# A hybrid decoder layer on one core: tables earlier, squares on one engine, factors spread by matmul

## The chip, the cores and the metric

The kernel runs on one core of a Trainium2 chip. What is compared is the device time of one launch in microseconds (us). The core has TensorE (PE in the profile; its weight loads are PEld), VectorE (DVE), ScalarE (ACT), GpSimd (POOL) and SyncE (SP), each with its own queue of instructions that run in the order in which they stand. SP and ScalarE also issue the DMAs.

## The reference

One layer over x (2048 rows of 1024 fp32 numbers): RMS norm, one input projection, three kinds of heads, a gate, an output projection, a second RMS norm and the residual. Cut to what matters here:

```python
def rmsnorm(x, g):
    xf = x.astype(jnp.float32)
    xf = xf * lax.rsqrt(jnp.mean(xf * xf, axis=-1, keepdims=True) + EPS)
    return (xf * g.astype(jnp.float32)).astype(x.dtype)
...
    h = rmsnorm(x, g_pre[i])
    proj = h @ w_in[i]
    val, gate = proj[..., :MIX_W], proj[..., MIX_W:]
    y_pool = pool_mixer(u_pool, w_pool[i], pool_scale[i])
    y_ssm = s5_mixer(u_ssm, a_re[i], a_im[i], log_dt[i], b_re[i], b_im[i],
                     c_re[i], c_im[i], d_skip[i], w_glu[i])
    y_att = memory_attention(q, mem, g_mem[i], w_kv[i])
    y = jnp.concatenate([y_pool, y_ssm, y_att], axis=-1) * jax.nn.silu(gate)
    x = x + rmsnorm(y @ w_out[i], g_post[i])
```

The pool heads take running means over 2, 4, 8 or 16 rows. The scan heads (`s5_mixer`) run a linear recurrence with 64 complex states for each of 24 groups; its powers and angles are tables made from a_re, a_im and log_dt. The attention heads read 256 memory rows, which are normed, too.

## The kernel before, in words

Every product is made from split operands: a number is the sum of a rounded high part (ScalarE, line 159) and the rest (VectorE or GpSimd, line 160), and `mm3` (lines 162 to 165) makes three multiplications of them. x is not divided by its root mean square ahead of the products. The row factors are made apart, and each product is multiplied by them when it leaves PSUM (`qf` of line 904, `gp` of 999, `up` of 1031), so that products can run before the factors are known.

The rows come in four chunks of 512. The first stage (to about 107 us) makes, for each chunk, the scan heads' part of the projection (`u_mm`, product `pu`), empties it (`us`) and stores it to DRAM (`ud`). Between these stand the keys and values of the memory (`kv_mm`, products `pkv`), the parameter tables (`param_tables`), the pool heads' weights folded into the projection's (`pool_fold`: a product `pf` in one of the two banks tagged mm, the copy `wpo` of line 358, a store to `wpd`), and the squares of all rows of x. `row_squares` (line 187) loads x again in 32 pieces of 128x512 and squares them with a sum along each row, the first half of each row tile on ScalarE and the second on VectorE.

`rstd_out` (line 223) makes the factors of all 2048 rows on VectorE (`row_rstd`, thirteen small steps, lines 170 to 203), turns them with one TensorE transposition (`rs_t`, line 227), and stores them to DRAM twice, in row order (`rsd`) and in the scan's order (`rsp`). `rs_load` then loads 512 of them into all 128 partitions (`rs_b`), and `rs_ct_load` loads the scan's copy (`rs_ct`). For the memory's rows another way is in use: `rstd_spread` (line 207) multiplies a column of factors, repeated 128 times, with the identity matrix, which leaves the factors along the free axis on all partitions, and ScalarE copies them out of PSUM.

`param_tables` works on all three elementwise engines: VectorE makes exponentials, GpSimd two halves of a table of angles in turns (`ph`, lines 472 to 479, in buffers that both halves share), VectorE its absolute value (`rd`, line 480), ScalarE sines and cosines (lines 484 and 485), VectorE from these `XT_` and `YT_` (lines 490 and 491).

The second stage (from about 107 to 515 us) runs through the queries (`pjq`), pool heads (`pjp`) and gates (`pjg`) of each half of the rows, in the two banks tagged mm. The steps of attention and of twelve scan blocks are put between them; a scan block's first product is `pa`, its inputs `uh` and `ul` come from `ur`, which GpSimd multiplies by `rs_ct`, and its last product `py` needs `hh` and `hl`. The third stage is the output projection.

The order is not that of the program. A scheduler with a timing model of its own places each engine's instructions, taking those that stand earlier in the program first where several could go. A line moved in the program so changes priorities, and with them the order of everything behind it.

The lines of the main sequence that the change touches, each on a line of its own in the listing:

```python
    kv_mm(1, wkv[1])
    wkv.append(kv_weight(3))
...
    row_squares(ssq_m, mem, range(NMEM // P), "rsm")
    kv_mm(2, wkv[2])
...
    vfs = kv_values(pkv[1], rm)
    param_tables()
...
    rstd_out()
    rs_load(0)
    rs_load(1)
    rs_ct_load()
```

Of the kernel before, what the change touches and what calls it, by code (L numbers as in the profile page):

```python
# [10 lines left out]
F32 = mybir.dt.float32  # L11
F32R = mybir.dt.float32r
I32 = mybir.dt.int32
AF = mybir.ActivationFunctionType
# [4 lines left out]
P = 128  # L19
# [63 lines left out]
def hybrid_layer_kernel(  # L83
# [53 lines left out]
    def aux_bank(name, shape=(P, CH)):  # L137
        return psum.tile(list(shape), F32, tag="aux", name=name, bufs=6)
# [49 lines left out]
    def row_squares(ss, rows, tiles, name):  # L188

        for i in tiles:  # L190
            for h in range(2):
                xr = t2k(f"{name}_x{i}_{h}")
                dma(xr, rows[i * P:(i + 1) * P, h * CH:(h + 1) * CH])
                if h:
                    dve.scalar_tensor_tensor(
                        xr, xr, 1.0, xr, op0=ALU.mult, op1=ALU.mult, accum_out=ss[:, h, i:i + 1]
                    )
                else:
                    act.activation(xr, xr, AF.Square, accum_out=ss[:, h, i:i + 1])

    def row_rstd(ss, nt, name):
        sm = small.tile([P, nt], F32, tag=f"rsu{nt}", name=f"{name}_sum", bufs=1)
        dve.tensor_tensor(sm, ss[:, 0, :], ss[:, 1, :], op=ALU.add)
        return rstd_from(sm, nt, name)

    def rstd_spread(r, n, dst, name):

        bc = aux_bank(f"{name}_bc", (P, n))
        for i in range(n // P):
            pe.matmul(  # L210
                bc[:, i * P:(i + 1) * P], r[:, i:i + 1].broadcast_to([P, P]), ident, start=True, stop=True
            )
        act.activation(dst, bc, AF.Copy)
# [9 lines left out]
    def rstd_out():  # L223

        r = row_rstd(ssq_x, NTT, "rs")
        rt_ = aux_bank("rs_t", (NTT, P))
        pe.transpose(rt_, r, ident)
        ro = small.tile([NTT, 2, P], F32, tag="rs_o", name="rs_o", bufs=1)
        act.activation(ro[:, 0, :], rt_, AF.Copy)
        act.activation(  # L230
            ro[:, 1, :].rearrange("i (s j) -> i s j", s=T),
            rt_.rearrange("i (j s) -> i s j", s=T)[:, ::-1, :],
            AF.Copy,
        )
        store(rsd, ro[:, 0, :])
        store(rsp.rearrange("s i j -> i s j"), ro[:, 1, :].rearrange("i (s j) -> i s j", s=T))

    def rs_load(c):
        rs_b[c] = const.tile([P, CH], F32, tag="rs_b", name=f"rs_b{c}", bufs=2)
        dma(rs_b[c], rsd[c * CH // P:(c + 1) * CH // P, :].rearrange("i p -> (i p)").partition_broadcast(P))  # L240
# [305 lines left out]
    def kv_weight(m, raw=None):  # L546
        return w_tile(w_kv[:, m * P:(m + 1) * P], f"wkv{m}", raw)

    def kv_mm(m, w):
        if m % 2 == 0:  # L550
            pkv[m // 2] = mm_bank(f"pkv{m // 2}", (P, 2, NMEM))
        o = pkv[m // 2][:, m % 2, :]
        for k in range(KT):
            mm3(o, w[0][:, k, :], w[1][:, k, :], mems[k][:, 0, :], mems[k][:, 1, :], k == 0, k == KT - 1)
# [55 lines left out]
    u_evac(2)  # L610
    kv_mm(0, wkv[0])
    wkv.append(kv_weight(2, ph1a))
    kv_mm(1, wkv[1])
    wkv.append(kv_weight(3))
    u_store(2)
    u_mm(3, [0])
    load_chunk(0, False)
    row_squares(ssq_m, mem, range(NMEM // P), "rsm")
    kv_mm(2, wkv[2])
    u_evac(3, [0])  # L620
    u_mm(3, [1])
    param_loads()
    rm_ = row_rstd(ssq_m, NMEM // P, "rsm")
    kv_mm(3, wkv[3])
    u_evac(3, [1])
# [10 lines left out]
    rstd_spread(rm_, NMEM, rm, "rsm")  # L636
    kv_keys(pkv[0], rm)
    vfs = kv_values(pkv[1], rm)
    param_tables()
    u_mm(0, [2])  # L640
    u_evac(0, [2])
    u_mm(1, [0])
# [5 lines left out]
    u_evac(1, [1])  # L648
    u_mm(1, [2], between=folds)
    rstd_out()  # L650
    rs_load(0)
    rs_load(1)
    rs_ct_load()
    u_evac(1, [2])
    u_store(1)
# [751 lines left out]
```

## Time and profile before

| | |
|---|---|
| median of 3 runs | 755.06 us (754.26 to 757.27) |
| the profiled execution's own time | 754.54 us |
| its span | 752.8 us |
| mean granted clock of TensorE | 0.98 |
| busy: TensorE, its weight loads | 708.1 us (94%), 575.9 us (77%) |
| busy: VectorE, ScalarE, GpSimd | 525.7 (70%), 337.4 (45%), 364.1 us (48%) |

The profiled execution is one run of the program; it lies 0.52 us below the median. Busy time is an average over stages with different limits. Where a row of the trace ends with square brackets, they hold the time for which the engine did nothing before this instruction, and what ended that.

### The profile page before, as it was taken

What the parts mean: (1) busy time and instruction counts of PE and PEld (TensorE: products, weight loads), DVE (VectorE), ACT (ScalarE), POOL (GpSimd) and SP (SyncE); (2) the same over time, 40 slices, a digit from 0 to 9 for tenths busy, and PEclk for the clock granted to TensorE, in tenths of its full rate; (3) what the DMA queues carried; (4) which work ended last, traced back from release to release, by engine and by line L of the source; (5) the groups of instructions that cost most, each with busy time, mean ns of one, the idle gap of its engine ahead of it and who ended that gap; (6) DMA issues with size and microseconds to landing.
All of it is one profiled execution on the core that took longest, in us unless ns stands there. A gap on an engine that the chain in (4) does not pass through costs nothing.

```text
span 752.8 us, 10077 instructions
## 1 busy us (share of the span) xinstructions
PE 708.1 (94%) x3449; PEld 575.9 (77%) x3449; DVE 525.7 (70%) x901; ACT 337.4 (45%) x731; POOL 364.1 (48%) x311
## 2 busy tenths in 40 slices
PE   6999787999979799888999999999999999999996
PEld 5788676887858588666888888888887888888885
DVE  4699594689889887978788978657606964343224
ACT  5675432557455453445555565447632524221111
POOL 0049852678758566846858488103042621421121
PEclk9999998999999899999999999999999999999999
DMA  7998985233333347482332324377725464330331
GB/s 252 309 328 270 336 288 156 98 108 126 121 114 119 112 150 247 161 280 83 122 107 71 121 81 154 134 224 275 226 80 192 130 199 123 113 126 14 112 113 56
DMA packets 95268, 121.03 MB, mean 161 GB/s; under 512 B 31585, under 2 KB 63025, under 8 KB 95217
## 3 DMA queue, kind: packets, MB, share of 16 engines
q1 hardware_dynamic: 82320, 90.08, 38.1%
q10 hardware_dynamic: 12896, 30.30, 10.6%
q8 instruction: 27, 0.44, 0.2%
q14 instruction: 25, 0.20, 0.1%
HBM read 81.68 MB, written 38.68 MB: 160 GB/s over the span
## 4 chain that ended last, share of the span: by engine, by line
PE 59%; DVE 13%; ACT 3%; issue 2%; DMA 1%; ACTq 0%; POOL 0%; DVEq 0%; POOLq 0%
PE pout L165 8%; PE pout L164 8%; PE pout L163 8%; PE pjg L163 5%; PE pjg L164 5%; PE pjg L165 5%; PE pz L163 2%; PE pz L165 2%; PE pz L164 2%; PE pjp L163 2%; PE pjp L164 2%; PE pjp L165 2%; DVE gg L847 2%; DMA ysd<-ys 1%; DVE yt L1007 1%
## 5 line engine op out<-in xcount | busy, mean ns | idle before, releaser
L163 PE MATMUL pjg<-xh,wg_h 128*128 128x512 f32 x256 | 103.6, 405 | 0.0
L164 PE MATMUL pout<-wol,yh 128*128 128x512 f32 (+1 forms) x264 | 102.0, 386 | 0.0
L164 PE MATMUL pjg<-xl,wg_h 128*128 128x512 f32 x256 | 101.9, 398 | 0.0
L165 PE MATMUL pjg<-xh,wg_l 128*128 128x512 f32 x256 | 101.7, 397 | 0.0
L163 PE MATMUL pout<-woh,yh 128*128 128x512 f32 (+1 forms) x264 | 101.6, 386 | 0.0
L165 PE MATMUL pout<-woh,yl 128*128 128x512 f32 (+1 forms) x264 | 101.2, 387 | 0.0
L1217 POOL TENSOR_TENSOR ov<-ov,xres 128x1024 f32<-128x1024 f32 x15 | 36.7, 2444 | 126.8 <-DVE ov L1216 105.0
L1213 ACT ACTIVATE ov<-pout 128x512 f32<-128x512 f32 x30 | 17.9, 596 | 105.3 <-PE pout L165 82.0
L163 PEld LDWEIGHTS pjg<-xh,wg_h 128*128 128x128 f32 x256 | 48.5, 189 | 12.8 <-issue 1.6
L164 PEld LDWEIGHTS pout<-wol,yh 128*128 128x128 f32 x264 | 49.5, 188 | 11.0
L163 PEld LDWEIGHTS pout<-woh,yh 128*128 128x128 f32 x264 | 49.5, 188 | 10.9
L165 PEld LDWEIGHTS pout<-woh,yl 128*128 128x128 f32 x264 | 49.5, 188 | 10.9
L165 PEld LDWEIGHTS pjg<-xh,wg_l 128*128 128x128 f32 x256 | 48.4, 189 | 11.3
L164 PEld LDWEIGHTS pjg<-xl,wg_h 128*128 128x128 f32 x256 | 48.7, 190 | 10.1
L160 POOL TENSOR_TENSOR yl<-yb,yh 128x512 fp32r<-128x512 f32 x20 | 26.9, 1375 | 60.6 <-ACT yh L159 39.7
L254 DVE SCALAR_TENSOR_TENSOR xl<-xr,gpre,xh 128x512 fp32r<-128x512 f32 x48 | 43.0, 908 | 18.7 <-ACT xh L253 18.6
L844 POOL TENSOR_TENSOR v<-v,ax 128x512 f32<-128x512 f32 x12 | 16.8, 1403 | 68.0 <-DVE ax L843 50.8
L253 ACT ACTIVATE xh<-xr,gpre 128x512 fp32r<-128x512 f32 x48 | 33.2, 715 | 32.4 <-DMA xr<-in_xT_dram 10.3
L163 PE MATMUL pu<-xh,wsh 128*128 128x512 f32 x96 | 39.0, 421 | 8.2 <-ACT wsh L159 6.8
L1185 DVE SCALAR_TENSOR_TENSOR ow<-ssq,ov 128x1 f32<-128x1 f32 x16 | 2.7, 168 | 54.7 <-ACT ov L1213 54.6
L163 PE MATMUL pjp<-xh,wp_h 128*128 128x512 f32 x96 | 39.0, 407 | 0.7 <-DVE gp L999 0.7
L164 PE MATMUL pu<-xl,wsh 128*128 128x512 f32 x96 | 38.7, 416 | 0.3 <-DVE xl L254 0.3
(300 smaller groups left out, 1929.3 us busy)
## 6 DMA issues: line engine op xcount, KB each, us to landing
xr<-in_xT_dram SPq DMA_DIRECT2D x32, 256.0 KB
rs_x<-in_x_dram SPq DMA_DIRECT2D x32, 256.0 KB
yd<-yt ACTq DMA_DIRECT2D x16, 512.0 KB
xres<-in_x_dram SPq DMA_DIRECT2D x16, 512.0 KB
out_dram<-ov SPq DMA_DIRECT2D x15, 512.0 KB
yb<-yd SPq DMA_DIRECT2D x20, 256.0 KB
wg_r<-in_w_in_dram SPq DMA_DIRECT2D x8, 512.0 KB
wsh<-wg_h ACTq DMA_DIRECT2D x8, 512.0 KB
```

Source lines behind the costliest of these rows:

```text
L160: sub.tensor_tensor(lo, src, hi.bitcast(F32), op=ALU.subtract)
L163: pe.matmul(ps, ahi, bhi, start=first, stop=False)
L164: pe.matmul(ps, ahi, blo, start=False, stop=False)
L165: pe.matmul(ps, alo, bhi, start=False, stop=last)
L253: act.activation(h, xr, AF.Copy, scale=gpre[:, k:k + 1])
L254: dve.scalar_tensor_tensor(l, xr, gpre[:, k:k + 1], h.bitcast(F32), op0=ALU.mult, op1=ALU.subtract)
L844: pool.tensor_tensor(v, v, ax, op=ALU.add)
L847: dve.tensor_tensor_scan(gg[:, i, :], r8[:, g0 + i:g0 + i + 1].broadcast_to([P, NJ]), v[:, i, :], 0.0, op0=ALU.mult, op1=ALU.add,)
L1007: dve.scalar_tensor_tensor(o, branch()[:, cc * CH:(cc + 1) * CH], 0.5, th, op0=ALU.mult, op1=ALU.mult)
L1185: dve.scalar_tensor_tensor(w, ssq[:, i:i + 1], 1.0 / D, v, op0=ALU.mult, op1=ALU.add)
L1213: act.activation(ov[:, HALVES[n]], ps[n], AF.Square, accum_out=ssq[:, n:n + 1])
L1217: pool.tensor_tensor(ov, ov, xr, op=ALU.add)
```

## The change

It does three things. `param_loads` and `param_tables` stand earlier in the program: the loads between the two products of the keys, the tables ahead of the values' first product. All squares are made by ScalarE, those of the memory's rows too. And the factors of chunks 0 and 1 are no longer loaded from DRAM but spread by `rstd_spread`, with four multiplications each, into the same tiles `rs_b`. The stores to DRAM stay, as the scan's copy and chunks 2 and 3 are still loaded from there.

```diff
@@ row_squares
                 dma(xr, rows[i * P:(i + 1) * P, h * CH:(h + 1) * CH])
-                if h:
-                    dve.scalar_tensor_tensor(
-                        xr, xr, 1.0, xr, op0=ALU.mult, op1=ALU.mult, accum_out=ss[:, h, i:i + 1]
-                    )
-                else:
-                    act.activation(xr, xr, AF.Square, accum_out=ss[:, h, i:i + 1])
+                act.activation(xr, xr, AF.Square, accum_out=ss[:, h, i:i + 1])
@@ rstd_out
         r = row_rstd(ssq_x, NTT, "rs")
+        for c in range(2):
+            rs_b[c] = const.tile([P, CH], F32, tag="rs_b", name=f"rs_b{c}", bufs=2)
+            rstd_spread(r[:, c * CH // P:(c + 1) * CH // P], CH, rs_b[c], f"rs{c}")
         rt_ = aux_bank("rs_t", (NTT, P))
@@ main sequence
     wkv.append(kv_weight(2, ph1a))
+    param_loads()
     kv_mm(1, wkv[1])
...
     row_squares(ssq_m, mem, range(NMEM // P), "rsm")
+    param_tables()
     kv_mm(2, wkv[2])
     u_evac(3, [0])
     u_mm(3, [1])
-    param_loads()
...
     vfs = kv_values(pkv[1], rm)
-    param_tables()
     u_mm(0, [2])
...
     rstd_out()
-    rs_load(0)
-    rs_load(1)
     rs_ct_load()
```

On TensorE 8 multiplications are new; ScalarE has 20 instructions more, VectorE 18 squares fewer, SP two loads fewer. What the scheduler makes of it shows at three places. The names with the last number taken as a buffer's are those of the program: `rd`, `ph`, `sin`, `cos` here belong to the second half of the tables.

VectorE around the second half of the tables, where the first folded weights (`wpo`) leave PSUM; before:

```order
L195 SCALAR_TENSOR_TENSOR rs_x_1_791,ssq_x<-rs_x_1_791 128x512
L195 SCALAR_TENSOR_TENSOR rs_x_1_797,ssq_x<-rs_x_1_797 128x512
L583 TENSOR_TENSOR vhl<-vt_1130,vhl 128x2x64
L583 TENSOR_TENSOR vhl<-vt_1137,vhl 128x2x64
L480 SCALAR_TENSOR_TENSOR rd_994<-ph_993 128x492
L583 TENSOR_TENSOR vhl<-vt_1130,vhl 128x2x64
L491 SCALAR_TENSOR_TENSOR YT__114<-sin_975,yk 128x216
L583 TENSOR_TENSOR vhl<-vt_1137,vhl 128x2x64
L358 COPY wpo_1156<-pf_1151 128x384
L490 TENSOR_TENSOR XT__113<-cos_976,yk 128x216
```

and with the change:

```order
L565 TENSOR_TENSOR vf_1050<-pkv_703,rm 128x256
L160 TENSOR_TENSOR kl<-kf_1044,kh 128x256
L478 SCALAR_TENSOR_TENSOR rd_645<-ph_644 128x492
L489 SCALAR_TENSOR_TENSOR YT__114<-sin_626,yk 128x216
L581 TENSOR_TENSOR vhl<-vt_1130,vhl 128x2x64
L581 TENSOR_TENSOR vhl<-vt_1137,vhl 128x2x64
L488 TENSOR_TENSOR XT__113<-cos_627,yk 128x216
L356 COPY wpo_1156<-pf_1151 128x384
```

The squares ahead of `rd` are gone, and the first `wpo` has moved behind `XT_`, which needs the cosines.

ScalarE at the same place, with the change (`rs_x` are the squares; before, six stood ahead of the sines, and they were every other one):

```order
L194 ACTIVATE rs_x_0_931,ssq_x<-rs_x_0_931 128x512
L194 ACTIVATE rs_x_1_934,ssq_x<-rs_x_1_934 128x512
L482 ACTIVATE sin_626<-ph_644 128x108
L482 ACTIVATE SIN<-ph_644,cs 128x384
L194 ACTIVATE rs_x_0_937,ssq_x<-rs_x_0_937 128x512
L580 ACTIVATE vhl<-vt_1130 128x2x64
L580 ACTIVATE vhl<-vt_1137 128x2x64
L483 ACTIVATE cos_627<-rd_645,cs 128x108
L483 ACTIVATE COS<-rd_645,cs 128x384
```

Eight squares stand ahead of the sines now, and 24 behind them.

TensorE at the end of the first query weight's products (`pjq`), where the factors come in; before:

```order
L164 MATMUL pjq_0_1_1412<-xl_5_724,wq_0_h 128x512
L227 MATMUL rs_t<-ident,rs_y_1284 16x128
L165 MATMUL pjq_0_1_1412<-xh_5_723,wq_0_l 128x512
...
L165 MATMUL pjq_0_1_1412<-xh_7_735,wq_0_l 128x512
L745 MATMUL pr_1338<-ident,rt_1331 128x128 x2
L754 MATMUL pk_1345<-ox_1326,rt_1331 16x128 x2
L163 MATMUL pjq_0_0_1495<-xh_0_488,wq_0_h 128x512
```

and with the change:

```order
L165 MATMUL pjq_0_1_1422<-xh_6_872,wq_0_l 128x512
L205 MATMUL rs_bc<-ident,rs_y_1284 128x128 x8
L225 MATMUL rs_t<-ident,rs_y_1284 16x128
L163 MATMUL pjq_0_1_1422<-xh_7_878,wq_0_h 128x512
L164 MATMUL pjq_0_1_1422<-xl_7_879,wq_0_h 128x512
L165 MATMUL pjq_0_1_1422<-xh_7_878,wq_0_l 128x512
L741 MATMUL pr_1348<-ident,rt_1341 128x128 x2
L750 MATMUL pk_1355<-ox_1336,rt_1341 16x128 x2
L163 MATMUL pjq_0_0_1505<-xh_0_502,wq_0_h 128x512
```

The eight new multiplications and the transposition stand four multiplications later, after 21 of the 24 of this product; the second query weight's first product still follows the first scan block's kernel (`pr`, `pk`).

## Rows read from the trace of the kernel before

**Rows 1.** Stretches: length, busy us of PE, PEld, DVE, ACT, POOL; clock, DMA share, GB/s
```profile
84.00:109.00 25.00, 19.13 (x103) 16.12 (x102) 19.94 (x45) 9.37 (x28) 13.88 (x14) 0.93 0.99 342
60.00:160.00 100.00, 90.21 (x445) 73.61 (x444) 74.24 (x127) 44.38 (x107) 65.80 (x62) 0.95 0.65 214
160.00:260.00 100.00, 89.26 (x480) 72.00 (x479) 90.64 (x119) 52.00 (x129) 72.21 (x59) 0.95 0.38 129
```

**Rows 2.** Whom TensorE waited for, 60 to 160 us (total, times, longest)
```profile
PE pf L356 <- DVE wpo L358: 4.3, 2, 3.9
PE pjq L163 <- DVE qf L904: 3.9, 1, 3.9
PE pjq L163 <- DVE wpo L358: 1.6, 1, 1.6
```

**Rows 3.** The stretches after the two long waits (columns as in rows 1)
```profile
91.30:95.20 3.90, 3.90 (x14) 3.33 (x15) 3.90 (x9) 2.40 (x7) 3.60 (x4) 0.57 1.06 377
123.40:129.30 5.90, 5.90 (x14) 4.66 (x15) 3.63 (x4) 1.86 (x3) 1.27 (x1) 0.50 0.80 268
```

**Rows 4.** VectorE in order of time (start, us, instruction; idle before it)
```profile
67.84 2.17 DVE L160 TENSOR_TENSOR wq_l<-wq_r,wq_h 128x1024 fp32r<-128x1024 f32 x1
69.93 1.08 DVE L304 COPY us<-pu 128x512 f32<-128x512 f32 x1
...
89.40 0.67 DVE L480 SCALAR_TENSOR_TENSOR rd<-ph 128x492 f32<-128x492 f32 x1 [4.94 <-POOL ph L479]
```

**Rows 5.** GpSimd in order of time, the second half of the tables
```profile
71.66 1.41 POOL L472 TENSOR_TENSOR ph<-fa,cs 128x492 f32<-128x492 f32 x1 [1.35 <-DVE rd L480]
...
76.16 1.41 POOL L522 TENSOR_TENSOR Bre<-br,cr 128x384 f32<-128x384 f32 x1
77.53 0.84 POOL L526 TENSOR_TENSOR Bim<-bi,cr 128x384 f32<-128x384 f32 x1
...
88.15 1.22 POOL L479 TENSOR_TENSOR ph<-ph,rd 128x492 f32<-128x492 f32 x1
```

**Rows 6.** The squares of x rows (ns min/median/max, first and last start)
```profile
L199 ACT ACTIVATE rs_x<-rs_x x16: 614/630/634, 75.3 to 107.5; 128x512 f32<-128x512 f32 x16
L195 DVE SCALAR_TENSOR_TENSOR rs_x<-rs_x x16: 668/758/1531, 76.2 to 107.0; 128x512 f32<-128x512 f32 x16
```

**Rows 7.** TensorE in order of time, the waits and the transposition
```profile
91.28 1.51 PE L356 MATMUL pf<-wp,wpt 96*128 96x96 f32 x8 [3.95 <-DVE wpo L358]
...
116.80 0.27 PE L227 MATMUL rs_t<-ident,rs_y 128*16 128x128 f32 x1
...
123.39 0.80 PE L163 MATMUL pjq<-xh,wq_h 128*128 128x512 f32 x1 [3.92 <-DVE qf L904]
```

**Rows 8.** VectorE in order of time, the factor chain's first and last
```profile
108.70 0.68 DVE L203 TENSOR_TENSOR rs_sum<-ssq_x 128x16 f32<-128x16 f32 x1
...
115.06 0.17 DVE L179 SCALAR_TENSOR_TENSOR rs_y<-rs_b,rs_y 128x16 f32<-128x16 f32 x1
```

**Rows 9.** ScalarE in order of time, a store's issue and two squares
```profile
91.26 0.33 ACTq L119 DMA_DIRECT2D wpd<-wpo  x1
91.69 0.63 ACT L199 ACTIVATE rs_x<-rs_x 128x512 f32<-128x512 f32 x1 [0.51 <-DVE XT__113 L490]
...
92.32 0.61 ACT L199 ACTIVATE rs_x<-rs_x 128x512 f32<-128x512 f32 x1
```

**Rows 10.** TensorE in order of time, the spread of the memory's factors
```profile
68.64 0.61 PE L210 MATMUL rsm_bc<-ident,rsm_y 128*128 128x128 f32 x4
69.01 0.47 PE L163 MATMUL pu<-xh,wsh 128*128 128x512 f32 x1
```

**Rows 11.** GpSimd in order of time, after a square, and after the factors
```profile
104.55 0.93 POOL L729 TENSOR_TENSOR cmbo<-Cim,YT__114 128x288 f32<-128x288 f32 x1 [1.39 <-ACT rs_x L199]
...
125.90 1.27 POOL L787 TENSOR_TENSOR ur<-ur,rs_ct 128x512 f32<-128x512 f32 x1 [3.90 <-DMA rs_ct<-rsp]
```

**Rows 12.** Whom TensorE waited for, 160 to 400 us, the longest
```profile
PE py L164 <- DVE hl L160: 10.6, 5, 3.9
```

## The prediction

> **What bounds the kernel now.** I read the stretches first [rows 1]. TensorE is the engine that sets the time almost everywhere, but not in all stretches alike: from 60 to 160 us it is busy for 90.21 of 100 us at a granted clock of 0.95, and from 160 to 260 us for 89.26, while VectorE there is busy for 90.64. The reader should see that time can be won in the idle places of TensorE, and that the change lies in the first of these two stretches. What TensorE waits for there is a short list [rows 2]: 4.3 us for the copies `wpo` that empty the folded pool weights from PSUM (two waits, the longest 3.9), 1.6 us for the same copies once more, and 3.9 us for `qf`, the first query product times its row factors. Nothing else. Each of the two long waits is followed by a stretch at a lower clock [rows 3]: 0.57 over 3.9 us after the first, 0.50 (the level of 1.2 GHz) over 5.9 us after the second. At the full clock that work would have taken 3.9 x 0.57 = 2.2 us and 5.9 x 0.50 = 2.95 us, so the clock costs 1.7 and 3.0 us. In all 4.3 + 1.6 + 1.7 + 3.9 + 3.0 = **14.5 us** are on offer, and no more.
>
> Why these waits? The first: VectorE stands for 4.94 us in front of `rd`, which needs GpSimd's last `ph` of the tables [rows 4], and the copy `wpo` stands behind it in VectorE's queue (the first piece of order in the section on the change). GpSimd's chain for that half starts at 71.66 us, after a wait of 1.35 us for VectorE's earlier `rd`, and its last step ends at 88.15 + 1.22 = 89.4 us [rows 5]. The short waits come since the copies alternate with squares of x rows on VectorE, of 0.67 to 1.53 us [rows 6]. The third long wait: the factor chain on VectorE runs from 108.70 to 115.2 us, and the factors then go by way of DRAM; the first query product that needs a free PSUM bank starts only at 123.39 us [rows 7, 8].
>
> **The change part by part.**
>
> *Loads of the parameters.* They are the same eight loads. In the order of SP most of them already stood at the same place; those of `Cim` and `dsk` move ahead of the memory rows. I cost this at nothing: the bytes are the same, and TensorE has no wait between 60 us and the first one named above.
>
> *Tables.* In the order GpSimd's queue is unchanged up to there. What moves is VectorE's side: the earlier `rd` no longer stands behind the split of the second query weight (2.17 us) and a copy of u (1.08 us) [rows 4], so GpSimd's last chain starts up to 3.2 us earlier. Its own length, 17.7 us, contains steps slowed beside VectorE: of two products of one shape one took 1.41 and the next 0.84 us [rows 5]. With sixteen squares fewer on VectorE I estimate 2.5 us less over the fourteen steps. That gives an end at 89.4 - 3.2 - 2.5 = 83.7 us. The bounds: 88.0 us, if only the wait of 1.35 us goes, and 83.7. I take 83.7, since both causes have their row. The first copy `wpo` now stands behind the sines, cosines and `XT` too: about 1.9 us from GpSimd's end to its done copy before (89.4 to the restart of TensorE at 91.28), 3.3 us now, hence 87.0 us. TensorE reaches that point at 91.28 - 3.95 = 87.3 us [rows 7]: the long wait goes and with it its low clock, and the short ones, as VectorE has only copies left: -4.3 - 1.6 - 1.7 = **-7.6 us**.
>
> *Squares.* Eighteen leave VectorE, the sixteen of x with a median of 0.76 us [rows 6], together 12 us; there they were partly in the way of the copies (counted above). They go to ScalarE, which squares in 0.63 us and starts the next 0.63 us later; one issue of a store costs it 91.69 - 91.26 = 0.43 us [rows 9]. In the order eight squares stand ahead of the sine of GpSimd's late half, and 24 behind it, with 12 issues: 24 x 0.63 + 12 x 0.43 + 2.4 (sines, cosines and four small copies, estimated from the 1.9 us between 89.4 and 91.26) = 22.7 us. The last square would end at 83.7 + 22.7 = 106.4 us, against 107.49 + 0.6 = 108.1 before [rows 6]. From 84 to 109 us VectorE was busy for 19.94 of 25 us and ScalarE for 9.37 [rows 1], so VectorE had room left. The Trainium skill (Perfetto Trace Analysis, section Optimizing Scalar/DVE Operations) advises giving such work to ScalarE if VectorE is saturated, which this row says it is not; by that rule the move puts ScalarE's queue in front of the factors and the sum is that of the first rival below, by the rows it is the forecast.
>
> *Factors.* The chain of thirteen small VectorE steps took 115.2 - 108.7 = 6.5 us [rows 8]; its last step took 0.17, so undisturbed it could be 2.3. I keep 6.5, the chain's own row: GpSimd's steps beside it (`cmbo` and what follows) waited for the buffers of late squares [rows 11], and will again. Factors ready: 106.4 + 0.2 + 6.5 = 113.1 us (bounds 108.9 and, with the tables late, 117.4). TensorE had passed the transposition of the factors at 116.80 us without a wait; it would come to the new spread, four multiplications of 0.23 us later in the order, at 116.8 - 7.6 + 0.9 = 110.1 us. **New wait: 113.1 - 110.1 = 3.0 us** (bounds 0 and 7.3). Behind it stand TensorE's whole queue, and behind the factors ScalarE's copies and VectorE's `qf`. The spread itself is eight multiplications; two of them took 69.01 - 68.64 = 0.37 us [rows 10], so **+1.5 us**. Its copy (0.63) and `qf` (0.69) run beside the rest of the spread, three multiplications, the transposition and the first block's kernel; that cover is 1.5 + 1.8 = 3.3 us (from 116.80 to 123.39 - 3.92 TensorE took 2.7 us for this and four multiplications more) against 0.75 + 0.63 + 0.69 = 2.1 us, and without it they would cost those 2.1 at most. The old wait of 3.9 us and its clock go: **-6.9 us**. Of the 3.0 us of clock some may come back after a new wait of 3.0; I charge half of the smaller price, **+0.9**.
>
> *Still by way of DRAM* go the factors in the scan's order (`rs_ct`). From the transposition to `ur` that uses them 9.1 us passed [rows 7, 11]. The transposition would be at 114.6; ScalarE now has two copies, a weight split and `qh` ahead of the stores, about 2.3 us more, but two loads of 256 KB leave SP's queue ahead of this one. `ur` at about 126, its halves at 127.8; TensorE comes to the scan's first product, 45 multiplications behind the second query product, at 113.1 + 1.5 + 1.8 + 45 x 0.233 = 126.9 us: **+1.0 us** (bounds 0 and 2.5). The loads of chunks 2 and 3 by `rs_load` stay as they are.
>
> Sum: -7.6 - 6.9 + 3.0 + 1.5 + 0.9 + 1.0 = **-8.1 us**. The profiled execution took 754.54 us (span 752.8), the median of the three runs is 755.06; -8.1 on the former is 746.4, which I give in the median's terms as **747 us**. Its own range by the bounds is 743 to 752. From 130 us on I take the shift as kept: the work is the same and all of it starts earlier.
>
> **The rivals.**
>
> *ScalarE becomes the bound.* If each of the 24 squares waits 0.2 us more for its row or for a copy ahead of a store, the factors come at 118 us, TensorE stands for 7.9 us and the clock falls as after the 3.9 us: -14.5 + 7.9 + 1.5 + 3.0 = -2.1, **753 us**. For it speaks that one in-order queue then carries squares, sines and stores; against it that ScalarE had 15.6 idle us from 84 to 109 [rows 1].
>
> *The tables are not earlier.* With GpSimd's end at 88.0 us the first wait stays (4.0 + 1.7), the last square comes at 110.7, the factors at 117.4, TensorE at 115.8: -14.5 + 5.7 + 1.6 + 1.5 + 1.0 = -4.7, **750 us**. For it: GpSimd's order is the same row for row; against it the 1.35 us it stood waiting [rows 5].
>
> *The scan's stage turns worse: slower.* From 160 to 400 us TensorE waits 10.6 us, five times, for `hl`, the last VectorE step before a scan block's output product, at most 3.9 us each [rows 12]. The scheduler has put VectorE's instructions in another order from there on: gate steps move ahead of `hl`, and TensorE's output products move back by some 12 multiplications (2.8 us) to match. VectorE has 9 us of slack in 100 [rows 1]. If `hl` slips by more than TensorE's own shift, each of the first half's seven blocks can wait. It decides at 8.1 us in all, 1.2 us per block, for no gain; at 1.9 us per block the end is **760 us**. Against it: the products stand later in TensorE's queue by more than the gate steps ahead of `hl` last.
>
> *The same stage turns better.* If those 12 multiplications take up half of the 10.6 us, the end is **741 us**. TensorE would then be ahead of the scan by less.
>
> **How the numbers follow.** Forecast 0.53, ScalarE as the bound 0.14, tables not earlier 0.08, scan worse 0.10, scan better 0.15. A measurement of this kernel can tell about 0.5% from no change, 3.8 us; so 751.3 and 758.8 are the limits. Faster: 0.53 + 0.15 + half of the tables' 0.08 = 0.72; the same: 0.14 + 0.04 = 0.18; slower: 0.10. The range of 739 to 756 us takes in the bounds, ScalarE as the bound and most of the better scan, and leaves out the slower case and the ends.
>
> **What would show it.** TensorE's waits from 60 to 160 us should no longer name `wpo` or `qf`, and name the factors `rs_y` (about 3 us) and `uh` (1 us). GpSimd's last `ph` should end near 84 us, the last square near 106, the first product of the second query weight should start near 116 us instead of 123.39, and the waits for `hl` should stay near 10 us. A `ph` ending after 87, a last square after 109, or waits for `hl` above 15 us would make the prediction wrong.

## The result and the profile after

| | before | changed |
|---|---|---|
| first comparison, median (lowest to highest) | 755.37 us (752.95 to 757.83, 7 runs) | 750.95 us (747.16 to 752.52, 7 runs) |
| ratio, 95% interval | | 0.9928 [0.9906, 0.9949] |
| the profiled execution, its span | 754.54, 752.8 us | 747.16, 745.3 us |

The kernel is faster by 0.7%, 4.4 us by the medians; the prediction said 747, by about 8 us. The profiled execution is the fastest of its seven. Two further comparisons of the same kernel gave 0.9948 and 0.9916 (runs e4 and e9 below), so by the medians all three lie between 4.1 and 6.3 us.

The stretches of the changed kernel, with the columns of [rows 1]:

```profile
84.00:109.00 25.00, 21.48 (x118) 17.72 (x117) 13.33 (x24) 17.95 (x57) 10.26 (x15) 1.00 0.98 348
60.00:160.00 100.00, 95.40 (x499) 77.52 (x498) 63.59 (x101) 58.58 (x148) 58.99 (x60) 1.00 0.68 226
160.00:260.00 100.00, 92.03 (x493) 74.52 (x492) 86.66 (x121) 56.15 (x140) 72.48 (x61) 0.95 0.36 120
```

From 60 to 160 us TensorE is busy for 5.2 us more than in [rows 1], in this execution at the full clock. VectorE and ScalarE have changed places from 84 to 109 us (13.33 and 17.95 us, against 19.94 and 9.37). Whom TensorE waited for from 60 to 160 us in the changed kernel (total, times, longest), which answers [rows 2]:

```profile
PE pf L354 <- DVE wpo L356: 3.3, 3, 1.4
PE pu L164 <- DVE xl L252: 0.8, 1, 0.8
...
PE pjq L163 <- DVE wpo L356: 0.2, 1, 0.2
```

The wait for `qf` is gone, and no wait for the factors has come in its place. The waits for the copies `wpo` have not gone: 3.5 us of 5.9 are left, in shorter pieces. They can be followed on TensorE, in order of time:

```profile
88.60 1.13 PE L354 MATMUL pf<-wp,wpt 96*128 96x96 f32 x8 [1.43 <-DVE wpo L356]
99.75 1.13 PE L354 MATMUL pf<-wp,wpt 96*128 96x96 f32 x8 [0.81 <-DVE wpo L356]
101.94 1.13 PE L354 MATMUL pf<-wp,wpt 96*128 96x96 f32 x8 [1.06 <-DVE wpo L356]
103.30 0.50 PE L163 MATMUL pjq<-xh,wq_h 128*128 128x512 f32 x1 [0.22 <-DVE wpo L356]
113.91 1.95 PE L205 MATMUL rs_bc<-ident,rs_y 128*128 128x128 f32 x16
117.36 0.50 PE L163 MATMUL pjq<-xh,wq_h 128*128 128x512 f32 x1
127.95 0.28 PE L163 MATMUL pa<-uh,rh 128*128 128x256 f32 x1
```

The second query weight's first product starts at 117.36 us instead of 123.39, with nothing idle ahead of it. VectorE in the same stretch:

```profile
85.63 0.67 DVE L478 SCALAR_TENSOR_TENSOR rd<-ph 128x492 f32<-128x492 f32 x1 [8.34 <-POOL ph L477]
87.99 0.55 DVE L356 COPY wpo<-pf 128x384 f32<-128x384 f32 x1
...
96.97 1.10 DVE L302 COPY us<-pu 128x512 f32<-128x512 f32 x1 [4.36 <-ACT rs_x L194]
...
99.16 0.53 DVE L356 COPY wpo<-pf 128x384 f32<-128x384 f32 x1
...
106.35 0.93 DVE L198 TENSOR_TENSOR rs_sum<-ssq_x 128x16 f32<-128x16 f32 x1 [2.65 <-ACT rs_x L194]
...
112.93 0.17 DVE L179 SCALAR_TENSOR_TENSOR rs_y<-rs_b,rs_y 128x16 f32<-128x16 f32 x1
```

Two things stand there. VectorE waits 8.34 us for GpSimd's last `ph`, more than the 4.94 of [rows 4]: it has less to do, and arrives earlier. And at 97 us it waits 4.36 us in front of a copy `us`, which empties a product of the first stage. `us` takes its buffer from the same ring (a set of buffers handed out in turns) as the x rows that are squared, so it needs a square of ScalarE to be over; the copies `wpo` stand behind it in VectorE's queue. GpSimd, in order of time:

```profile
69.72 1.03 POOL L470 TENSOR_TENSOR ph<-fa,cs 128x492 f32<-128x492 f32 x1 [3.28 <-DVE rd L478]
...
84.37 1.23 POOL L477 TENSOR_TENSOR ph<-ph,rd 128x492 f32<-128x492 f32 x1
...
121.21 1.29 POOL L783 TENSOR_TENSOR ur<-ur,rs_ct 128x512 f32<-128x512 f32 x1 [0.80 <-issue]
```

### The profile page after: what moved, and what is told of

Same layout as the page of the kernel before. It is cut to its first block, busy times and chain, and to the rows that moved or that the text cites. A ratio compares the mean times of both kernels' runs of the same rounds, so it can differ in the third digit from the quotient of the medians.

```text
span 745.3 us, 10113 instructions
## 1 busy us (share of the span) xinstructions
PE 709.3 (95%) x3465; PEld 576.2 (77%) x3465; DVE 500.5 (67%) x865; ACT 349.0 (47%) x769; POOL 356.7 (48%) x311
## 4 chain that ended last, share of the span: by engine, by line
PE 65%; DVE 18%; DMA 6%; issue 4%; ACT 3%; POOL 2%; ACTq 0%; SPq 0%; DVEq 0%; POOLq 0%
PE pout L165 8%; PE pout L164 8%; PE pout L163 8%; PE pjg L163 6%; PE pjg L165 6%; PE pjg L164 6%; DMA xr<-in_xT_dram 3%; DVE xl L252 2%; PE pz L163 2%; PE pz L164 2%; PE pz L165 2%; DVE gg L843 2%; PE pjp L165 2%; PE pjp L163 2%; PE pjp L164 2%
## 5 line engine op out<-in xcount | busy, mean ns | idle before, releaser
L251 ACT ACTIVATE xh<-xr,gpre 128x512 fp32r<-128x512 f32 x48 | 32.9, 714 | 27.5 <-DMA xr<-in_xT_dram 13.5
```

What stands on the lines that cost most here:

```text
L251: act.activation(h, xr, AF.Copy, scale=gpre[:, k:k + 1])
```

## The experiments

The kernels were compared in three groups (e1 to e4, e5 to e8, e9 to e12), each with its own runs of the kernel before beside it. The first three and e5 to e7 take the change apart. Medians in us, ratios to the kernel before:

| kernel | spread | squares | tables | median | ratio, interval | first `pjp` |
|---|---|---|---|---|---|---|
| e1 | yes | | | 752.70 | 0.9973 [0.9953, 0.9993] | 136.0 |
| e2 | | yes | | 752.29 | 0.9978 [0.9963, 0.9993] | 134.1 |
| e3 | | | yes | 756.64 | 1.0030 [1.0012, 1.0048] | 140.6 |
| e5, e10 | yes | yes | | 748.81, 747.33 | 0.9914 [0.9896, 0.9933], 0.9901 [0.9869, 0.9934] | 130.4, 133.7 |
| e6 | | yes | yes | 757.59 | 1.0031 [1.0017, 1.0044] | 137.4 |
| e7 | yes | | yes | 751.95 | 0.9964 [0.9950, 0.9978] | 134.6 |
| e4, e9 | yes | yes | yes | 750.54, 749.10 | 0.9948 [0.9929, 0.9967], 0.9916 [0.9891, 0.9940] | 132.9, 132.6 |

The median of before was 754.61, 754.95 and 755.43 us beside the three groups. The last column is the start of the first pool-head product in one profiled execution of each, which shows how far the front (all that stands ahead of it on TensorE) has moved; before it was 139.2 us. Two executions of one kernel differ by up to 3.3 us there (e5 and e10), so single differences of that size tell little.

**e1, the spread alone.**

```diff
         r = row_rstd(ssq_x, NTT, "rs")
+        for c in range(2):
+            rs_b[c] = const.tile([P, CH], F32, tag="rs_b", name=f"rs_b{c}", bufs=2)
+            rstd_spread(r[:, c * CH // P:(c + 1) * CH // P], CH, rs_b[c], f"rs{c}")
...
-    rs_load(0)
-    rs_load(1)
```

> The spread alone: the factors of chunks 0 and 1 by multiplication, everything else as before. Theory (the trip through DRAM is what the front waits for last): the first product of the second query weight starts at 120 to 122 us instead of 123.39, no stretch at 1.2 GHz follows, the first pool-head product starts at 133 to 135 us instead of 139.2, and the time falls by 4 to 6 us. The waits for the weight copies stay at 5 to 6 us. Rival (three equal parts of the measured 4.4 us): 1.5 us less. Rival (only the three together pay): no change.

It gained 1.9 us, where 4 to 6 were expected; the first pool-head product came at 136.0 us, not at 133 to 135. Whom TensorE waited for from 60 to 160 us:

```profile
PE pf L359 <- DVE wpo L361: 5.0, 1, 5.0
PE pjq L163 <- DVE wpo L361: 1.4, 1, 1.4
```

The wait for `qf` is gone, so the spread does what it says. The wait for the copies is still there, and the first one is longer than in [rows 2] (5.0 against 3.9). That is not the spread's doing: this wait lies ahead of it, TensorE's order up to there is that of the kernel before, and in this execution TensorE only came to it earlier, at 85.4 us instead of 87.3.

**e2, the squares alone.**

```diff
-                if h:
-                    dve.scalar_tensor_tensor(
...
-                else:
-                    act.activation(xr, xr, AF.Square, accum_out=ss[:, h, i:i + 1])
+                act.activation(xr, xr, AF.Square, accum_out=ss[:, h, i:i + 1])
```

> The squares alone on ScalarE. Theory: the last square stays within 1.5 us of 108 us, as ScalarE now stands in front of the late sines with squares behind it, so the factors, the trip through DRAM and the first pool-head product stay within 1.5 us of before (139.2 us); the waits for the weight copies shrink by 2 to 4 us but TensorE then waits longer for the first query factors. Time within 2 us of before. Rival (the squares carry the gain): waits for the weight copies gone and 3 to 4 us less in all.

It gained 2.3 us. TensorE's waits from 60 to 160 us:

```profile
PE pjq L163 <- DVE qf L899: 4.4, 1, 4.4
PE pf L351 <- DVE wpo L353: 1.5, 2, 1.3
PE pjq L163 <- DVE wpo L353: 0.2, 1, 0.2
```

VectorE's wait for the tables, in order of time:

```profile
86.71 0.67 DVE L475 SCALAR_TENSOR_TENSOR rd<-ph 128x492 f32<-128x492 f32 x1 [8.43 <-POOL ph L474]
```

The expectation was a time within 2 us of before; the median lies just beyond that, and the interval (0.5 to 2.8 us) doesn't decide. What it said of the front fell: the last square ended at 105.4 us and the first pool-head product started at 134.1, 5.1 us earlier, where 1.5 at most were expected. With the tables where they stood, VectorE's `rd` starts at 86.71 us instead of 89.40 [rows 4], and the copies' long wait is gone. The wait for `qf` is 4.4 us, only 0.5 more than in [rows 2], since the factors come earlier, too: their transposition is at 112.36 us instead of 116.80.

**e3, the tables alone.**

```diff
+    param_loads()
     kv_mm(1, wkv[1])
...
+    param_tables()
     kv_mm(2, wkv[2])
...
-    param_loads()
...
-    param_tables()
```

> The tables alone earlier. Theory: GpSimd's last table step ends 2 to 4 us earlier than 89.4, the long wait for the weight copies shrinks from 3.9 to 1 or 2 us, but the last square stays at 107 to 108 and so the factors by way of DRAM and the first pool-head product (139.2 us) move by less than 1.5 us. Time within 2 us of before. Rival (the tables carry the gain): first pool-head product 3 to 4 us earlier, and so the end.

It was slower, by 0.3%. TensorE's waits from 60 to 160 us:

```profile
PE pf L356 <- DVE wpo L358: 5.1, 3, 3.7
PE pjq L163 <- DVE qf L904: 3.7, 1, 3.7
PE pjq L163 <- DVE wpo L358: 0.7, 1, 0.7
```

The stretch behind the last of them (columns as in [rows 1]):

```profile
106.00:112.00 6.00, 5.28 (x16) 4.27 (x16) 5.93 (x12) 1.68 (x5) 5.07 (x8) 0.50 0.68 220
```

Both long waits are there, and 1.2 GHz is granted from 106 to 112 us, where the kernel before had the full clock. GpSimd's last `ph` ends at 88.1 us, 1.3 us earlier than before: without the squares' move, the tables' move brings no more than that, and in e1, where the tables stand as before, the end came 0.9 us earlier, too.

**e4, the changed kernel once more.**

> The changed kernel once more, unaltered. Theory: the front is the same in every execution (first pool-head product within 0.5 us of 130.8), and the spread of its times, 747 to 752.5 us, is made later, by the waits of the scan blocks and the clock after them from 160 to 400 us. Rival: the front itself varies by 2 us or more between executions.

750.54 us. Its profiled execution took 750.67 us, with the same order and a front that is slower by 2 us: its first pool-head product starts at 132.9 us, that of the first profile at 130.8. The theory fell, and the rival holds: the front itself varies by 2 us. The reason is the clock. TensorE's waits of this execution in order of time, against 88.60, 99.75 and 101.94 us in the first one:

```profile
87.38 1.13 PE L354 MATMUL pf<-wp,wpt 96*128 96x96 f32 x8 [1.25 <-DVE wpo L356]
99.62 1.13 PE L354 MATMUL pf<-wp,wpt 96*128 96x96 f32 x8 [1.89 <-DVE wpo L356]
101.83 2.02 PE L354 MATMUL pf<-wp,wpt 96*128 96x96 f32 x8 [1.08 <-DVE wpo L356]
```

The two waits near 100 us end within 0.13 us of where they ended in the first execution, and yet the spread, with nothing idle on the way, starts at 115.95 us instead of 113.91. The stretch from 100 to 106 us, first of this execution, then of the first one:

```profile
100.00:106.00 6.00, 4.92 (x21) 4.28 (x21) 3.67 (x6) 4.93 (x15) 2.46 (x4) 0.56 1.00 372
```

```profile
100.00:106.00 6.00, 4.72 (x28) 3.89 (x28) 3.70 (x6) 4.81 (x15) 2.34 (x4) 1.00 1.06 393
```

In the first one TensorE had waited 0.81 and 1.06 us for copies near 100 us, and kept the clock. In this one it waited 1.89 and 1.08 us at the same places, and made 21 multiplications in a stretch where the other made 28. So what is left of the copies' waits costs more than its own length in some executions. The same rows show that the second wait ends at a time that TensorE doesn't set: here TensorE left the first wait 1.2 us sooner, and stood 1.1 us longer at the second.

**e5, squares and spread without the tables' move.**

> Squares on ScalarE and the spread by TensorE, the parameter loads and tables left where they stood. Theory A (the tables' move gives nothing; taking the squares off VectorE is what lets the copies wpo run, and the spread is what removes the wait for qf): the two gains of the parts alone add up, -2.3 - 1.9 = -4.2 us, a time of about 750.4 us, not to be told from the whole change; the waits of TensorE from 60 to 160 us are those for wpo (about 2 us as in the squares alone) and none for qf; the first pool-head product starts near 131 us. Theory B (the tables' move pays, but only with the squares gone from VectorE): this kernel loses what the tables give, 752 us or more, GpSimd's last ph ends near 87 us as with the squares alone, and the whole change is faster by 1.5 us or more.

748.81 us, a gain of 6.1 us: theory A, and more than the sum of the parts. TensorE's waits from 60 to 160 us:

```profile
PE pf L354 <- DVE wpo L356: 1.7, 2, 1.5
...
```

VectorE in order of time, at the end of the tables:

```profile
85.18 0.67 DVE L478 SCALAR_TENSOR_TENSOR rd<-ph 128x492 f32<-128x492 f32 x1 [8.43 <-POOL ph L477]
```

`rd` starts at 85.18 us with the tables unmoved, and at 85.63 with them moved. In the three profiles of the changed kernel it starts at 84.41 to 85.63 us, so the tables' move brings nothing here that can be told.

**e6, squares and tables without the spread.** The parts of e2 and e3 together.

> Squares on ScalarE and the tables moved; the factors by way of DRAM as before. Theory A (the tables' move gives nothing): as the squares alone, 752.3 us, or slower by up to the 2 us that the move cost alone; the wait for qf stays at about 4 us. Theory B (the move pays with the squares gone): 750.8 us or less, GpSimd's last ph ends near 85 us as in the whole change, and the wait for wpo is below that of the squares alone (1.9 us).

757.59 us: slower than before, and its interval lies wholly above that of the squares alone. Theory B is out. TensorE's waits from 60 to 160 us:

```profile
PE pjq L163 <- DVE qf L899: 4.6, 1, 4.6
PE pf L351 <- DVE wpo L353: 2.9, 3, 1.3
...
```

The stretch of its last copies:

```profile
100.00:106.00 6.00, 4.71 (x23) 3.82 (x22) 3.54 (x6) 4.97 (x16) 2.50 (x4) 0.81 1.05 395
```

Against the squares alone there are 1.4 us more of waits for copies, a lower clock behind them (0.81; the squares alone had 1.00), and the transposition of the factors stands four multiplications later in TensorE's order. It comes at 115.28 us instead of 112.36, and the way by DRAM starts with it. That accounts for a front that is 3.3 us later than in e2, but not for a time above that of the kernel before, as the front is still 1.8 us earlier than there. The rest is lost behind it: from the first pool-head product to the end it took 617.0 us here, 615.4 in e2 and 613.6 in the kernel before. What takes it there, no run shows.

**e7, spread and tables without the squares.** The parts of e1 and e3 together.

> The spread and the tables' move, the squares of x still half on VectorE. Both theories: the tables' move shows its cost, since its VectorE steps stand among the squares; by theory A (parts add up) 754.61 - 1.9 + 2.0 = 754.7 us, and TensorE's waits for wpo from 60 to 160 us stay at 4 us or more; by theory B also about 754 to 755 us. A rival for both: the cost of the tables alone came from later factors (the first product of the second query weight at 126 us instead of 123.4), and the spread takes that away: then 752.7 us as the spread alone.

751.95 us, the rival's number (752.7) rather than 754.7. The copies' waits are 4.8 and 1.6 us. With the spread in place the way by DRAM no longer holds TensorE, and the tables' move costs nothing that can be told.

**e8, own buffers for the two halves of the tables,** on the whole change.

```diff
-            ph, rd, pb = (ph1a.tile(shp, F32, tag=n, name=f"{n}{q}") for n in ("ph", "rd", "pb"))
+            ph, rd, pb = (ph1a.tile(shp, F32, tag=n if n == "pb" else f"{n}{q}", name=f"{n}{q}") for n in ("ph", "rd", "pb"))
```

> The whole change, and the two halves of the tables get own buffers for ph and rd, so that GpSimd need not wait 3.28 us at 69.7 us for VectorE's rd and ScalarE's sines of the first half. If GpSimd's chain is what holds the first copies wpo, its last ph ends at about 82.3 us instead of 85.6, the wait for the first copies (1.4 us) goes, and the time falls by 1.5 to 2.5 us against the whole change, to about 748.5 us; the later waits (0.8 and 1.1 us), which stand where two banks are emptied in turn, stay. Rival: those copies alternate with TensorE in two banks whatever the tables do, what is won at 88 us is lost at 100 us, and the time stays at 750.5 us. A second rival: GpSimd's steps then run beside more of VectorE's and are slower by as much.

749.91 us, ratio 0.9935 [0.9915, 0.9954]: not to be told from the whole change. The trace shows what the rival forecast, by a cause that it didn't name. VectorE in order of time:

```profile
81.80 1.46 DVE L478 SCALAR_TENSOR_TENSOR rd<-ph 128x492 f32<-128x492 f32 x1 [4.47 <-POOL ph L477]
...
96.20 1.10 DVE L302 COPY us<-pu 128x512 f32<-128x512 f32 x1 [4.94 <-ACT rs_x L194]
```

TensorE's waits for the copies, 60 to 160 us:

```profile
PE pf L354 <- DVE wpo L356: 2.5, 2, 1.4
```

The tables end 3.8 us earlier and the first wait of TensorE is gone. What it won at 88 us it gives back near 100 us (1.39 and 1.12 us), where VectorE stands 4.94 us in front of `us`; the clock from 100 to 106 us is 0.72 in this execution.

**e9 and e10, the whole change and the kernel without the tables' move on one chip.**

> The changed kernel as it is, for a comparison on one chip with the run that leaves the tables where they stood. Theory A (the tables' move costs what it costs alone, about 2 us): 750.6 us, slower than the next run by 1 to 2.5 us. Theory B (the two are the same kernel within what can be told): within 0.7 us of the next run.

> Squares and spread without the tables' move, the same kernel as run e5. Theory A: 748.8 us, faster than the whole change by 1 to 2.5 us; TensorE's waits for wpo are again one of 1.5 us and two of 0.2, where the whole change has 0.8 to 1.9 at each of the two places near 100 us. Theory B: the 748.8 of before was luck, and it now comes within 0.7 us of the whole change.

749.10 us (747.46 to 750.38) and 747.33 us (746.48 to 752.16), six runs each. The medians differ as theory A said, by 1.8 us, but the runs overlap and the two intervals of the ratio do, too. The profile of e10 shows 3.5 us of waits for copies, of which one is 1.9 us near 100 us: the short waits of e5 were one execution's. Theory A's expectation about the waits fell, and whether the tables' move costs 1 us or more in the whole change is not settled. It can be said that it brings nothing: squares and spread alone are at least as fast, with a smaller edit.

**e11, own buffers for the copies of u,** on the whole change.

```diff
-        us = t2k(f"us{m}_{c}", (P, T, CH // T))
+        us = (ph1a.tile([P, T, CH // T], F32, tag="usx", name=f"us{m}_{c}", bufs=2) if c < 2 and (m, c) != (0, 0)
+              else t2k(f"us{m}_{c}", (P, T, CH // T)))
```

> The whole change, and the copies us of chunks 0 and 1 get two buffers of their own instead of turns in the ring that the squared rows go through. Theory C (VectorE stood 4.36 us at 97 us since its copy us needed a buffer that ScalarE's late square had to free, and the copies wpo stood behind it): no us copy waits for a square any more, TensorE's waits for wpo near 100 us (0.8 and 1.1 us) go, with the low clock that follows them in some executions, and the time falls by 1.5 to 3 us against the whole change. Rival: the copies then wait for the products pu or for a store, the factors at 113 us take over as the bound of TensorE (a wait for rs_y of 1.5 to 2 us shows), and the gain is under 1 us.

749.51 us, ratio 0.9925 [0.9896, 0.9953]: no difference to e9. No `us` waits for a square any more, and TensorE waits for no `wpo` at all. Its waits from 60 to 160 us:

```profile
PE rs_bc L205 <- DVE rs_y L179: 2.9, 1, 2.9
PE vt L575 <- DVE vf L566: 2.3, 1, 2.3
...
```

VectorE in order of time, where the factors begin:

```profile
110.24 0.18 DVE L198 TENSOR_TENSOR rs_sum<-ssq_x 128x16 f32<-128x16 f32 x1 [4.86 <-ACT rs_x L194]
```

So it was `us` that kept the copies from TensorE. A wait for the factors came in its place, as the rival said, but it doesn't show that the factors are the next bound: they are later here, at 117.0 us instead of 113.1, since ScalarE began its squares at 81 us instead of 75.4. It stood 7.81 us in front of a store's issue and a split, and what held it there the trace doesn't tell clearly. TensorE came to the spread at 114.2 us (117.09 - 2.85), after 2.3 us at `vt`; factors at 113.1 us would not have held it, and without the wait at `vt` by 1.2 us at most.

**e12, squares shared again,** with e8's buffers on e5.

```diff
-                act.activation(xr, xr, AF.Square, accum_out=ss[:, h, i:i + 1])
+                if name == "rs" and h and i % 4 == 3:
+                    dve.scalar_tensor_tensor(
+                        xr, xr, 1.0, xr, op0=ALU.mult, op1=ALU.mult, accum_out=ss[:, h, i:i + 1]
+                    )
+                else:
+                    act.activation(xr, xr, AF.Square, accum_out=ss[:, h, i:i + 1])
```

> Squares and spread without the tables' move; four of the sixteen right half rows go back to VectorE, and the halves of the tables have own buffers for ph and rd. If ScalarE's 32 squares set when the factors come, and GpSimd's chain when the first copies come, then the last square ends near 104 us, the factors are ready near 110 us instead of 112.3, the first wait for wpo (1.5 us) goes, and the time is 1 to 2 us below that of squares and spread alone, about 747.3 us. Rival: the four squares stand ahead of copies in VectorE's queue again, at 0.76 us or more each, and the copies wait for them: no gain, 749 to 750 us.

752.56 us, ratio 0.9960 [0.9944, 0.9976]: it gives back some 3.5 us of what e5 had won, and 5.2 us against e10 in the same group. The last square came at 108.6 us, not 104, though ScalarE had four fewer. Whom ScalarE waited for from 76 to 112 us, first in e12, then in the changed kernel:

```profile
ACT rs_x L199 <- DMA rs_x<-in_x_dram: 6.5, 4, 2.4
ACT rs_x L199 <- DVE wpo L361: 2.6, 2, 2.1
```

```profile
ACT rs_x L194 <- DMA rs_x<-in_x_dram: 4.7, 8, 1.0
```

With four squares fewer ScalarE was not the busier for it: it stood 9.1 us, 6.5 for rows and 2.6 for which the profile names a copy `wpo` of VectorE. The expectation that ScalarE's number of squares sets the last one fell here. That the rows alone set it is not shown either. In e2, where all squares are ScalarE's, they waited for rows only 0.5 us in this stretch, and in the changed kernel the last seven ran without a gap:

```profile
101.91 0.63 ACT L194 ACTIVATE rs_x<-rs_x 128x512 f32<-128x512 f32 x1 [0.94 <-DVE wpo L356]
...
105.61 0.61 ACT L194 ACTIVATE rs_x<-rs_x 128x512 f32<-128x512 f32 x1
```

## Why the prediction was right, and where it was not

The kernel is faster, as forecast, and its front moved by the forecast amount in the profiled execution: the first pool-head product starts at 130.8 us instead of 139.2, 8.4 us earlier, against a sum of 8.1. The group of these products, before and in the changed kernel (min/median/max in ns, first and last start):

```profile
L163 PE MATMUL pjp<-xh,wp_h x96: 392/396/775, 139.2 to 432.4; 128*128 128x512 f32 x96
```

```profile
L163 PE MATMUL pjp<-xh,wp_h x96: 392/396/628, 130.8 to 423.9; 128*128 128x512 f32 x96
```

But that sum holds two errors that cancel, and the median kept only 4.4 us of it. By its steps:

*Tables.* The end of the tables was put at 83.7 us and came at 85.60, between the bounds. Both terms came out smaller: the earlier `rd` started 1.9 us sooner (68.92 against 70.85), not 3.2, and GpSimd's chain took 15.9 us instead of 17.7, 1.8 less and not 2.5. The first cause failed: `rd` starts at 68.67 us in e5, where the tables are not moved. In e3, where they are moved and the squares are not, the end is at 88.1 us. It was taking the squares off VectorE that freed GpSimd's chain: from the start of the earlier `rd` to the end of the tables it took 18.1 to 18.5 us in the four kernels with squares on VectorE (before, e1, e3, e7), tables moved or not, and 16.5 to 16.7 in e2, e5, e6, e10 and the three profiles of the changed kernel.

*Copies, -7.6 us: the step that failed.* The first query product starts at 103.30 us instead of 107.14, behind the last of the waits of [rows 2], so the term measured -3.8 us. Of the 3.5 us of waits that are left, 1.43 stand in front of the first copy, where the tables ended 1.9 us later than summed, and 2.1 near 100 us. The sentence at fault is "as VectorE has only copies left". It had, but one kind of them, `us`, needs buffers that the squares free. With all squares in one in-order queue on ScalarE, VectorE waits for that queue, and TensorE for VectorE. Run e8 shows that earlier tables don't help against it, and e11 that TensorE's waits for `wpo` go when `us` has buffers of its own.

*Squares.* The last was put at 106.4 us and ended at 106.2, by luck: the sines came 1.9 us later than summed, and from there on it took 20.6 us instead of 22.7. The 12 issues of stores, put at 5.2 us in a row, run beside the squares where nothing is waited for; 3.6 us of waits and gaps, for rows above all and for copies, stand in their place. The prediction also misread [rows 1] where it gave VectorE room. Nearly all that VectorE was idle from 84 to 109 us is the one wait of 4.94 us in front of `rd`; behind it, in the kernel before, it was busy for 19.48 of 19.60 us (columns as in [rows 1]):

```profile
89.40:109.00 19.60, 15.79 (x84) 13.59 (x85) 19.48 (x41) 8.79 (x25) 8.69 (x10) 0.91 1.01 361
```

The Trainium skill (Perfetto Trace Analysis, section Optimizing Scalar/DVE Operations) says that such a move may make sense if VectorE is saturated. Taken by stretches the trace agrees: in this one VectorE was, and the move alone gained 2.3 us (e2).

*Factors.* They were ready at 113.1 us, as predicted, with the luck of the last square. The new wait of 3.0 us was not there, since TensorE reached the spread at 113.91 instead of 110.1: the 3.8 us that the copies kept are the wait that the factors didn't cost. Taken together the two terms were put at -4.6 us and measured -3.8. From the spread to the second query weight's first product 3.45 us passed; the terms gave 1.5 + 1.8. The clock behind the old wait, priced at 3.0 us, gave back about 2.3: from the second query weight's first product to the first pool-head product it took 15.8 us before and 13.5 after.

*Scan's input, +1.0 us.* TensorE's first scan product at 127.95 us follows without a wait. From the issue of the store `rsp` (117.09 us) to `ur` 4.1 us passed, against 125.90 - 117.83 = 8.1 us before [rows 11]; the estimate of "two loads less" was too small.

*Clock.* Half of a price of 1.7 us was charged. The first profile shows none, e4 and e9 show it: 0.56 and 0.78 from 100 to 106 us, with the first pool-head product at 132.9 and 132.6 us. By the three profiles the front is 6.3 to 8.4 us earlier.

*The shift kept from 130 us on.* Not quite: from the first pool-head product to the end it took 613.6 us before (752.8 - 139.2) and 614.5, 615.9 and 615.0 us in the three profiles of the changed kernel. That is 0.9 to 2.3 us given back, against the only profile of the kernel before; in the kernels that hold one or two of the parts it is 614.1 (e7) to 617.0 us (e6). TensorE's waits from 135 to 400 us add up to 17.5 us before and 14.5, 17.1 and 17.1 us after; in the first of these the clock from 260 to 400 us is 0.96 instead of 0.99. So most of these waits only changed their names. From 160 to 400 us the longest groups of the changed kernel's first profile are these, against [rows 12]:

```profile
PE py L164 <- DVE hl L160: 6.3, 4, 4.0
PE pjq L163 <- DMA wq_h<-wsh: 2.2, 1, 2.2
...
```

Less of `hl`, more of the query weights: the scan's stage took neither of the turns that the rivals gave it. Which step gives the 0.9 to 2.3 us back, and how much of it is the change's, stays open; no run was aimed at it.

*The rivals.* "ScalarE becomes the bound" came closest to what happened, by another road than the one it named: its queue held VectorE's copies, not the factors. "The tables are not earlier" did not come: its end of 88.0 us is what the tables' move gives by itself (88.1 in e3), and the squares' move brought it to 85.6.

*Do the parts add up?* By the medians they don't: alone, the spread and the squares gain 1.9 and 2.3 us, together 6.1 and 8.1 (e5, e10). But the noise is of that size: by the intervals the two parts give 1.8 to 5.6 us when added up (the two half widths taken together as the root of the sum of their squares), and e5 alone 5.1 to 7.9. In the front of the profiled executions they do add up, 3.2 and 5.1 us alone against 8.8 and 5.5 together. Alone, each keeps less of it to the end. What takes it behind the front is not shown.

## What to carry to other kernels

When a wait ends at a time that another engine sets, what was won ahead of it is lost in front of it: in e4 TensorE left one wait 1.2 us sooner than in another execution and stood 1.1 us longer at the next. So before a wait is counted as gone, look up what ends the next one. An average busy share can hide a full stretch: 19.94 of 25 us were 19.48 of 19.60 behind one long wait. Before an operation is moved to an engine with room, look up who shares its buffers: a copy that takes turns in the ring of the moved operation's tiles waits for the new engine's queue. And an edit in a bundle can be dead weight, so time the bundle without each of its parts: here two of the three parts give all that the three do, and the third costs 0.3% alone and some 0.5% beside the second.

## What was not expected of the hardware

*Loads ahead of a small dependent load.* With the two 256 KB loads of `rs_b` ahead of `rs_ct` in SP's queue, 5.9 us passed from the issue of the load of `rs_ct` to `ur` in the kernel before (119.96 to 125.90); without them 2.7 us in e1 (123.32 to 126.06) and 3.1 in e7 (121.92 to 124.99). In these three the profile names that load as what ended the wait. In e2 and e3, with the loads, it was 5.8 us, but the rows name a store as the last to come. Of these, e1 differs from the kernel before in the spread only; no run changed the order of the loads alone.

*One kernel, two clocks.* In three executions of the changed kernel the two waits near 100 us took 0.81 and 1.06 us, 1.23 and 1.07, 1.89 and 1.08, and the clock from 100 to 106 us was 1.00, 0.78 and 0.56; the last two have fronts that are some 2 us later. The length of these two waits doesn't settle it: in e6 they took 0.60 and 1.07 us, and the clock was 0.81.

*DMA engines full for 36 us.* From 70 to 106 us, while the rows are loaded for the squares, the DMA share is 0.99 before and 1.04 in the changed kernel (columns as in [rows 1]):

```profile
70.00:106.00 36.00, 31.27 (x161) 26.07 (x159) 28.16 (x59) 16.17 (x45) 24.46 (x23) 0.95 0.99 335
```

```profile
70.00:106.00 36.00, 32.48 (x173) 26.77 (x172) 16.09 (x29) 24.99 (x77) 21.17 (x23) 1.00 1.04 367
```

The squares waited for rows at times (4.7 us in the changed kernel), so the transfers hold them part of the way. They are not shown to set the last square: the last seven ran without a gap (e12 above), and the loads in their turn need buffers that the squares free (in the changed kernel SP stood for squares nine times from 60 to 112 us, 3.2 us in all). No run loaded fewer bytes.
